# Hybrid attention/RWKV block on one core: the mixing's split weights kept in DRAM, loaded in a ring of three, and its stores on other queues

## The chip, the core and the metric

The kernel runs on one core of a Trainium2 chip. A core has a matrix engine (PE, whose weight loads are shown as PEld), a vector engine (DVE), a scalar engine (ACT), a general engine (POOL), and SP, which here only issues DMA transfers; ACT and POOL can issue them too. Each engine works through its own instructions in the order in which they were built, and waits where an operand is not there yet. The transfers of all issuers run on the same 16 DMA engines. The metric is the device time of one execution in microseconds (us). Three runs of the kernel before took 3460.87, 3462.41 and 3465.66 us.

## The reference

One layer over 2048 tokens of width 1024, in float32:

```python
h    = rms_norm(x, pre_mix_g)
proj = h @ w_in                      # 1536 attention, 1792 RWKV and 2048 gate columns
y_a  = chunk_band_attention(q, k, v, rel_bias)
y_b  = rwkv7_time_mix(p_rwkv, ...)   # recurrence over time, 8 heads of 64
merged = sigmoid(gate_a) * (y_a @ proj_a) + sigmoid(gate_b) * (y_b @ proj_b)
x = x + rms_norm(merged @ w_out, post_mix_g)
u = square(relu(rms_norm(x, pre_ffn_g) @ w_up)) @ w_down
x = x + rms_norm(u, post_ffn_g)
```

proj_a and proj_b are 512 x 1024, w_out is 1024 x 1024, w_up and w_down are 1024 x 4096 and 4096 x 1024.

## The kernel before

The tokens are cut into four groups of 512 (`G`). `run` (L1206) takes each group through `phase_rwkv`, `phase_attention` and `phase_merge`, which is called the mixing here, and then does the feed-forward part for two groups at a time (`phase_up`, `phase_down`).

**Precision.** A product is made of three: an operand is split into a rounded part `hi` and the rest `lo` (`split`, L68: a cast on ACT, a subtraction on DVE), and `mm3` (L72) adds hi x hi, hi x lo and lo x hi in PSUM. A block of 128 output columns for 512 tokens over 1024 inputs is thus 24 matmuls of 128x512.

**Weights of the mixing.** `wsplit` (L57) loads a block of weights raw through SP's queue (L62) and splits it (L69 on ACT writes `whi`, L70 on DVE writes `wlo`). Raw, hi and lo have two buffers each. It serves `dense` (L82: blocks of `w_in`, 14 for RWKV, 16 for the gates, 12 for attention), `branch` (L923: 8 blocks of `proj_b`, then 8 of `proj_a`, 256 KB each) and the loop over `w_out` in `phase_merge` (L955: 16 blocks of 256 KB). Each group does all of it anew: the same weights are loaded and split four times.

**The RWKV part.** `rwkv_pre` prepares a pair of heads, with one bonus product (L429) that waits for r (L427) and the products ps_A (L473). `rwkv_inverse` (L493) is a chain of 31 steps, two DVE instructions each (L506, L512), that ends with two transposes (L515, L517); `rwkv_blocks` starts with the products ps_t (L536), which wait for X of L515. Dense blocks of the gates (`gate`, L660) fill PE's time beside these chains. `mix` (L287) needs a carry column that POOL copies (L293, L294); `mN` (L394) is POOL's too.

**Stores and reloads.** Much is handed on through DRAM: the gates (`gd`, L665), the bonus (`bvd`, L431), the outputs of RWKV (`yd`, L658), keys and values for the next group (`kc`, `vc`, L797 and L798), branch b (`md`, L908), the mixing's output (`od`, L1231) and the residual's results (`x1`, L985; `ht`, L998; `td`, L1020). All of these go through SP's queue, among the loads.

**The merge.** `branch` loads a gate block `th` (L927, two buffers of 512 columns), multiplies y by a block of proj_a or proj_b (ps_p) and applies the gate on DVE (L932). Branch b is done beside the attention and stored in `md`; branch a then adds it back (`mb`, L946). After that come w_out's products (ps_o, L959), and beside them, as `between`, the norm of the next group (`phase_norm`, with transposes pstr, L115) and the residual of the group before (`residuals`, L968, with transposes ps_ht, L995). `rstd` (L91) runs on POOL.

**Order.** The program's order on each engine is not that of the source: when the program is built, instructions are ranked so that those whose inputs are expected earlier stand earlier. A change in one place thus moves instructions in others.

Of the kernel before, what the change touches and what calls it, by code (L numbers as in the profile page):

```python
# [17 lines left out]
P = 128  # L18
# [4 lines left out]
NP = 4  # L23
# [26 lines left out]
class Block:  # L50
# [31 lines left out]
    def dense(self, col):  # L82

        wh, wl = self.wsplit(
            self.a["w_in"][:, col : col + P].rearrange("(k p) n -> p k n", p=P), "w", KB, P
# [35 lines left out]
    def constants(self, ctx, mixing):  # L121
# [3 lines left out]
        dp = ctx.enter_context(tc.tile_pool(name="scratch", bufs=1, space=DRAM))  # L125
# [130 lines left out]
        self.gd = [dp.tile([P, G], F32, name=f"gd{i}") for i in range(2 * KB)]  # L256
        self.md = [dp.tile([P, G], F32, name=f"md{i}") for i in range(KB)]
# [81 lines left out]
    def rwkv_pre(self, g, p, rp, NA, between=lambda: None):  # L339
# [91 lines left out]
        nc.sync.dma_start(self.bvd[p], r)  # L431
# [192 lines left out]
    def rwkv_post(self, p, R):  # L624
# [33 lines left out]
        nc.sync.dma_start(self.yd[p], yf)  # L658

    def gate(self, i):  # L660
# [4 lines left out]
        nc.sync.dma_start(self.gd[i], t)  # L665
# [90 lines left out]
    def att_pair(self, g, p):  # L756
# [39 lines left out]
        if not lastg:  # L796
            nc.sync.dma_start(self.kc[p], KK[:, :, 1].bitcast(F32))  # L797
            nc.sync.dma_start(self.vc[p], VV[:, 1].bitcast(F32))  # L798
# [85 lines left out]
    def phase_attention(self, g):  # L884
# [5 lines left out]
        with ExitStack() as ctx:  # L890
# [16 lines left out]
            for i in range(KB):  # L907
                nc.sync.dma_start(self.md[i], self.branch(y, 1, i))  # L908
# [14 lines left out]
    def branch(self, y, br, i):  # L923

        nc, mp = self.nc, self.bp
        t = mp.tile([P, G], F32, tag="th", name="th")
        nc.sync.dma_start(t, self.gd[br * KB + i])  # L927
# [4 lines left out]
        nc.vector.scalar_tensor_tensor(t, t, 1.0, ps, op0=ALU.add, op1=ALU.mult)  # L932
        return t

    def phase_merge(self, g, o, between, early=iter(())):

        tc, nc, a = self.tc, self.nc, self.a
        with ExitStack() as ctx:
# [5 lines left out]
            for i in range(KB):  # L944
# [344 lines left out]
```

## Time and profile before

| | |
|---|---|
| median of three runs | 3462.41 us |
| profiled execution | 3462.33 us, of which the span from first to last instruction is 3460.6 us |
| mean granted TensorE clock | 0.985 |
| PE, PEld, DVE, ACT, POOL busy | 96%, 77%, 70%, 41%, 10% |
| DMA | 481.14 MB, 139 GB/s over the span |
| groups 0 to 3 of the mixing | about 0 to 520, 520 to 1060, 1060 to 1597, 1597 to 2118 us |
| feed-forward part | about 2118 to 3460 us |

The profile lists for each engine the busy time, and before what it sat idle. A row of the waits reads "who waits, in which line, for whom: us in total, times, longest". A row of a window gives, for a stretch of the span, each engine's busy time with its instructions, then the granted clock (1.00 is full), the DMA engines' mean busy share and the GB/s moved. A group of instructions is shown as line, engine, operation, "output<-inputs", shape and count, then busy time and mean ns of one, then the engine's idle time before them with what ended it. Matmuls are pipelined: one of 128x512 is shown with some 390 ns, though the next one starts some 0.23 us after it.

### The profile page before, as it was taken

To read this page: it belongs to the slowest core of one execution; us is meant where nothing else is said; L and a number is where in the kernel's file an instruction comes from. 1 tells how busy PE (TensorE), PEld (TensorE's weight loads), DVE (VectorE), ACT (ScalarE), POOL (GpSimd) and SP (SyncE) were. 2 spreads that over 40 slices of the span, in tenths; PEclk is the share of its full clock that TensorE was granted. 3 is DMA by queue.
4 is the path that set the end of the run, shared out by engine and by line. 5 is a ranking of instruction groups with operands and counts; after the bars stand their busy time and mean duration, and the time that the engine had idled before them with its cause. 6 is when DMAs were issued, how large, how long until landed. Compare 5 with 4: busy or idle time off the path is not lost. (4 is left out here: it accounts for less than half of the span.)

```text
span 3460.6 us, 50793 instructions
## 1 busy us (share of the span) xinstructions
PE 3310.7 (96%) x19233; PEld 2677.4 (77%) x19233; DVE 2421.3 (70%) x4206; ACT 1429.6 (41%) x2399; POOL 352.7 (10%) x700
## 2 busy tenths in 40 slices
PE   7999999999998999999999979999999999999998
PEld 5777777777877777877777867888888878888886
DVE  5774856766856765865774875777887788766667
ACT  4434634436644445644435635333331143331112
POOL 2210002100003110002210000111100021100001
PEclk9999999999999999999999999999999999999999
DMA  5223453225365225365224277334845374343333
GB/s 147 82 86 125 130 182 119 62 89 186 111 223 161 62 92 159 122 226 163 82 86 134 81 232 254 125 120 143 271 175 188 109 239 129 113 152 98 98 98 110
DMA packets 430124, 481.14 MB, mean 139 GB/s; under 512 B 19564, under 2 KB 322864, under 8 KB 429880
## 3 DMA queue, kind: packets, MB, share of 16 engines
q1 hardware_dynamic: 419640, 444.34, 40.2%
q0 software_dynamic: 10240, 33.56, 2.6%
q8 instruction: 151, 2.47, 0.3%
q14 instruction: 93, 0.76, 0.1%
HBM read 356.16 MB, written 124.81 MB: 139 GB/s over the span
## 5 line engine op out<-in xcount | busy, mean ns | idle before, releaser
L78 PE MATMUL ps_dn<-fop 128*128 128x512 f32 x3072 | 700.1, 390 | 0.9 <-DVE u L1169 0.9
L78 PEld LDWEIGHTS ps_dn<-fop 128*128 128x128 f32 x3072 | 575.9, 188 | 121.3 <-DVE u L1169 1.3
L78 PE MATMUL psd<-hh,whi 128*128 128x512 f32 x1344 | 546.4, 407 | 16.7 <-ACT whi L69 13.5
L78 PE MATMUL psd<-hl,whi 128*128 128x512 f32 x1344 | 544.9, 405 | 0.0
L78 PE MATMUL psd<-hh,wlo 128*128 128x512 f32 x1344 | 541.4, 403 | 0.7 <-DVE wlo L70 0.5
L69 ACT CAST whi<-wraw 128x1024 fp32r<-128x1024 f32 (+1 forms) x296 | 255.6, 864 | 578.2 <-PE psd L78 392.3
L70 DVE TENSOR_TENSOR wlo<-wraw,whi 128x1024 fp32r<-128x1024 f32 (+1 forms) x296 | 292.6, 989 | 264.9 <-ACT whi L69 200.4
L1169 DVE TENSOR_TENSOR u<-u,ps_dn 128x512 f32<-128x512 f32 x480 | 322.5, 684 | 152.8 <-PE ps_dn L78 152.0
L78 PEld LDWEIGHTS psd<-hh,whi 128*128 128x128 f32 x1344 | 258.3, 192 | 71.7 <-ACT whi L69 15.5
L78 PEld LDWEIGHTS psd<-hh,wlo 128*128 128x128 f32 x1344 | 258.0, 192 | 52.5 <-DVE wlo L70 3.5
L78 PEld LDWEIGHTS psd<-hl,whi 128*128 128x128 f32 x1344 | 258.6, 192 | 48.8
L69 ACT CAST fop<-wdraw 128x1024 fp32r<-128x1024 f32 x64 | 67.1, 1049 | 427.5 <-DVE u L1169 321.9
L1090 POOL DMA_DIRECT2D ad<-r x128 | 69.4, 543 | 683.8 <-DVE r L1089 683.8
L78 PE MATMUL ps_p<-yh,whi 128*128 128x512 f32 x256 | 107.8, 421 | 29.8 <-DVE th L932 17.8
L69 ACT CAST s12h<-s 128x1024 fp32r<-128x1024 f32 x32 | 33.7, 1054 | 185.1 <-PE ps_u L78 185.1
L826 DVE CUSTOM_DVE_ANT_0 sc<-bias,ps_s 128x640 f32<-128x640 f32 (+4 forms) x128 | 93.3, 729 | 22.4 <-PE ps_pt L838 13.0
L831 ACT ACTIVATE sc<-sc,mn 128x640 f32<-128x640 f32 (+4 forms) x128 | 97.8, 764 | 22.4 <-DVE mn L826 21.7
L78 PE MATMUL ps_p<-yh,wlo 128*128 128x512 f32 x256 | 105.4, 412 | 1.6 <-DVE wlo L70 1.6
L959 PE MATMUL ps_o<-whi,mh 128*128 128x512 f32 x256 | 98.6, 399 | 7.7 <-ACT whi L69 6.8
L78 PE MATMUL ps_p<-yl,whi 128*128 128x512 f32 x256 | 105.3, 412 | 0.0
L843 DVE TENSOR_TENSOR PTl<-ps_pt,PTh 128x640 fp32r<-128x640 f32 (+4 forms) x128 | 94.1, 735 | 12.9 <-ACT PTh L842 12.2
L959 PE MATMUL ps_o<-wlo,mh 128*128 128x512 f32 x256 | 102.1, 399 | 1.1 <-DVE wlo L70 1.1
(345 smaller groups left out, 6566.9 us busy)
## 6 DMA issues: line engine op xcount, KB each, us to landing
wraw<-in_w_in_dram SPq DMA_DIRECT2D x168, 512.0 KB
wraw<-in_w_up_dram SPq DMA_DIRECT2D x80, 512.0 KB
ad<-r POOLq DMA_DIRECT2D x128, 256.0 KB, 2.5
wdraw<-in_w_down_dram SPq DMA_DIRECT2D x64, 512.0 KB
araw<-ad SPq DMA_DIRECT2D x64, 512.0 KB
gd<-gate SPq DMA_DIRECT2D x64, 256.0 KB
th<-gd SPq DMA_DIRECT2D x64, 256.0 KB
wraw<-in_w_out_dram SPq DMA_DIRECT2D x64, 256.0 KB
```

The lines of the kernel that those rows point to most:

```text
L69: self.nc.scalar.copy(hi, src)
L70: self.nc.vector.tensor_tensor(lo, src, hi.bitcast(F32), ALU.subtract)
L78: mm = nc.tensor.matmul(ps, l, r, start=n == 0, stop=n == last).ins
L826: nc.vector.tensor_tensor_reduce(sc[:, 0:n], bias[:, s0:640], pss[:, c0 : c0 + n], 1.0, 3.0e38, ALU.add, ALU.min, mn,)
L831: nc.scalar.activation(sc[:, 0:n], sc[:, 0:n], AF.Exp, scale=-1.0, bias=mn, accum_out=sm)
L843: nc.vector.tensor_tensor(lv, pst[:, 0:nk], hv.bitcast(F32), ALU.subtract)
L959: nc.tensor.matmul(ps[t], l[:, k, ts], r[:, 0], start=k == 0 and j == 0, stop=k == KB - 1 and j == 2)
L1090: nc.gpsimd.dma_start(self.ad[fb][:, th], r)
L1169: nc.vector.tensor_tensor(u[t][:, ns], u[t][:, ns], ps, ALU.add)
```

## The change

Group 0 loads and splits each weight as before and in addition stores its two parts in DRAM (`kept`): hi through ACT's queue, lo through POOL's. Groups 1 to 3 load both parts with one transfer into one tile `w` and split nothing. All weight tiles now hold 1024 values a partition and part (`branches` makes two of the former blocks of 128 columns at once, the loop over w_out takes two blocks of rows), so that there are 58 of them in a group: 42 of w_in, 4 of proj_b, 4 of proj_a and 8 of w_out. The pool of the weights is opened after the first norm, with two buffers each of raw, hi and lo for group 0; it is closed before group 1 and opened again with three buffers of the double tile (24 KB a partition in both cases). Its buffers are released tile by tile.

The gate blocks, `md` and `mb` come in pairs too. The stores leave SP: bvd, yd, kc, vc, md, x1 and td go to POOL's queue, gd, od and ht to ACT's.

```diff
-    def wsplit(self, src, tag, k, n, raw_tag="raw", bufs=2):
+    def wsplit(self, src, k, n, key):
         nc = self.nc
-        w = self.wp
-        raw = w.tile([P, k, n], F32, tag=raw_tag, name="wraw")
+        if key in self.kept:
+            w = self.wp.tile([P, 2, k, n], F32R, tag="w", name="wsp")
+            nc.sync.dma_start(w.bitcast(F32), self.kept[key])
+            return w[:, 0], w[:, 1]
+        raw = self.wp.tile([P, k, n], F32, tag="raw", name="wraw")
         nc.sync.dma_start(raw, src)
-        hi = w.tile([P, k, n], F32R, tag=tag + "h", bufs=bufs, name="whi")
-        lo = w.tile([P, k, n], F32R, tag=tag + "l", bufs=bufs, name="wlo")
+        hi, lo = (self.wp.tile([P, k, n], F32R, tag="w" + x, name="w" + x) for x in ("hi", "lo"))
         self.split(hi, lo, raw)
+        d = self.kept[key] = self.dp.tile([P, 2, k, n], F32, name="kept_%s%d" % key)
+        nc.scalar.dma_start(d[:, 0], hi.bitcast(F32))
+        nc.gpsimd.dma_start(d[:, 1], lo.bitcast(F32))
         return hi, lo
...
-        self.gd = [dp.tile([P, G], F32, name=f"gd{i}") for i in range(2 * KB)]
-        self.md = [dp.tile([P, G], F32, name=f"md{i}") for i in range(KB)]
+        self.gd = [dp.tile([P, 2, G], F32, name=f"gd{i}") for i in range(KB)]
+        self.md = [dp.tile([P, 2, G], F32, name=f"md{i}") for i in range(KB // 2)]
...
-        nc.sync.dma_start(self.bvd[p], r)
+        nc.gpsimd.dma_start(self.bvd[p], r)
...
-        nc.sync.dma_start(self.gd[i], t)
+        nc.scalar.dma_start(self.gd[i // 2][:, i % 2], t)
...
-            for i in range(KB):
-                nc.sync.dma_start(self.md[i], self.branch(y, 1, i))
+            for i in range(KB // 2):
+                nc.gpsimd.dma_start(self.md[i], self.branches(y, 1, i))
...
-    def branch(self, y, br, i):
+    def branches(self, y, br, i):
-        nc, mp = self.nc, self.bp
-        t = mp.tile([P, G], F32, tag="th", name="th")
-        nc.sync.dma_start(t, self.gd[br * KB + i])
-        w = self.a[("proj_a", "proj_b")[br]][:, i * P : (i + 1) * P]
-        wh, wl = self.wsplit(w.rearrange("(k p) n -> p k n", p=P), "w", NP, P)
-        ps = self.pd.tile([P, G], F32, tag="d", name="ps_p")
-        self.mm3(ps, [(wh[:, k], wl[:, k], y[0][:, k], y[1][:, k]) for k in range(NP)])
-        nc.vector.scalar_tensor_tensor(t, t, 1.0, ps, op0=ALU.add, op1=ALU.mult)
+        nc = self.nc
+        t = self.bp.tile([P, 2, G], F32, tag="th", name="th")
+        nc.sync.dma_start(t, self.gd[br * KB // 2 + i])
+        w = self.a[("proj_a", "proj_b")[br]][:, 2 * i * P : (2 * i + 2) * P]
+        wh, wl = self.wsplit(w.rearrange("(k p) n -> p k n", p=P), NP, 2 * P, ("ab"[br], i))
+        for j in range(2):
+            c = slice(j * P, (j + 1) * P)
+            ps = self.pd.tile([P, G], F32, tag="d", name="ps_p")
+            self.mm3(ps, [(wh[:, k, c], wl[:, k, c], y[0][:, k], y[1][:, k]) for k in range(NP)])
+            nc.vector.scalar_tensor_tensor(t[:, j], t[:, j], 1.0, ps, op0=ALU.add, op1=ALU.mult)
         return t
...
-                advance(early, i % 2)
+                advance(early, 1)
...
                 for k in range(KB):
-                    wh, wl = self.wsplit(a["w_out"][k * P : (k + 1) * P, None, n * 512 : (n + 1) * 512], "w", 1, 512)
+                    if k % 2 == 0:
+                        rows = a["w_out"][k * P : (k + 2) * P, n * 512 : (n + 1) * 512]
+                        wh, wl = self.wsplit(rows.rearrange("(k p) n -> p k n", p=P), 2, 512, ("out", n * KB + k))
...
-            self.wp = e(tc.tile_pool(name="w", bufs=2))
...
+            weights = e(ExitStack())
             for g in range(self.NG):
+                if g < 2:
+                    weights.close()
+                    self.wp = weights.enter_context(tc.tile_pool(name="w", bufs=2 + g, reuse_waits="tile"))
...
-                        self.nc.sync.dma_start(self.od[g][t], o[t])
+                        self.nc.scalar.dma_start(self.od[g][t], o[t])
```

More of the change, by code (lines that the diff above doesn't have):

```diff
@@ L84, in dense @@
         wh, wl = self.wsplit(
-            self.a["w_in"][:, col : col + P].rearrange("(k p) n -> p k n", p=P), "w", KB, P
+            self.a["w_in"][:, col : col + P].rearrange("(k p) n -> p k n", p=P), KB, P, ("in", col)
         )
@@ L124, in constants @@
         cp = mixing.enter_context(tc.tile_pool(name="mconst", bufs=1, side="right"))
-        dp = ctx.enter_context(tc.tile_pool(name="scratch", bufs=1, space=DRAM))
+        dp = self.dp = ctx.enter_context(tc.tile_pool(name="scratch", bufs=1, space=DRAM))
+        self.kept = {}
         self.ident = keep.tile([P, P], F32, name="ident")
@@ L657, in rwkv_post @@
         nc.vector.tensor_tensor(yf, yf, ps, ALU.mult)
-        nc.sync.dma_start(self.yd[p], yf)
+        nc.gpsimd.dma_start(self.yd[p], yf)
     def gate(self, i):
@@ L796, in att_pair @@
         if not lastg:
-            nc.sync.dma_start(self.kc[p], KK[:, :, 1].bitcast(F32))
-            nc.sync.dma_start(self.vc[p], VV[:, 1].bitcast(F32))
+            nc.gpsimd.dma_start(self.kc[p], KK[:, :, 1].bitcast(F32))
+            nc.gpsimd.dma_start(self.vc[p], VV[:, 1].bitcast(F32))
         ya = ap.tile([P, G], F32, tag="ya", name="ya")
@@ L943, in phase_merge @@
             ml = cp.tile([P, KB, G], F32R, name="ml")
-            for i in range(KB):
-                mb = self.bp.tile([P, G], F32, tag="mb", name="mb")
+            for i in range(KB // 2):
+                mb = cp.tile([P, 2, G], F32, tag="mb", bufs=2, name="mb")
                 nc.sync.dma_start(mb, self.md[i])
-                t = self.branch(self.ya, 0, i)
+                t = self.branches(self.ya, 0, i)
                 nc.vector.tensor_tensor(t, t, mb, ALU.add)
-                self.split(mh[:, i], ml[:, i], t)
-                advance(early, i % 2)
+                self.split(mh[:, 2 * i : 2 * i + 2], ml[:, 2 * i : 2 * i + 2], t)
+                advance(early, 1)
             self.yctx.close()
@@ L959, in phase_merge @@
                             nc.tensor.matmul(
-                                ps[t], l[:, k, ts], r[:, 0], start=k == 0 and j == 0, stop=k == KB - 1 and j == 2
+                                ps[t], l[:, k, ts], r[:, k % 2], start=k == 0 and j == 0, stop=k == KB - 1 and j == 2
                             )
@@ L1019, in combinations @@
                 nc.vector.tensor_tensor(b[:, o], b[:, x], b[:, y], ALU.subtract)
-            nc.sync.dma_start(self.td[half][:, :, k], b)
+            nc.gpsimd.dma_start(self.td[half][:, :, k], b)
             yield
```

4 lines of the change are left out of this document (2 added, 2 removed).

## The prediction

> **What bounds the kernel now.** I read the page's head first, then the windows of the four groups, then who PE waited for in groups 1 to 3, then the instructions that the change removes.
>
> ```profile
> span 3460.6 us, 50793 instructions
> PE 3310.7 (96%) x19233; PEld 2677.4 (77%) x19233; DVE 2421.3 (70%) x4206; ACT 1429.6 (41%) x2399; POOL 352.7 (10%) x700
> ```
> ```profile
> 0.00:520.00 520.00, 481.50 (x3189) 379.48 (x3190) 336.76 (x742) 241.35 (x462) 61.67 (x130) 0.98 0.40 125
> 520.00:1060.00 540.00, 517.25 (x3488) 414.99 (x3487) 364.01 (x709) 271.64 (x482) 65.19 (x129) 0.99 0.43 138
> 1060.00:1597.00 537.00, 507.84 (x3431) 406.85 (x3430) 360.93 (x704) 266.44 (x476) 61.57 (x128) 0.98 0.42 136
> 1597.00:2118.00 521.00, 482.77 (x3284) 385.07 (x3283) 350.24 (x696) 242.79 (x429) 47.14 (x97) 0.96 0.42 132
> 2118.00:3460.60 1342.60, 1321.37 (x5847) 1091.04 (x5845) 1009.40 (x1358) 407.40 (x554) 117.10 (x216) 1.00 0.45 149
> ```
> The columns of the windows are length, then busy time of PE, PEld, DVE, ACT and POOL, the granted clock, the DMA share and GB/s. PE is the bound at 96%. The last row is the feed-forward part, which the change reaches only through the queue of a few stores; at full clock I leave it at nothing. The first four rows are the groups of the mixing. No other engine is near full there: DVE 64.8% to 67.4%, DMA 0.40 to 0.43. So the removal of work on ACT and DVE pays only where PE waited for it, or where the clock was lowered behind a wait. In groups 1 to 3 the clock rows give 0.01 x 540 + 0.02 x 537 + 0.04 x 521 = 37 us of clock time not granted (rounded rows: some 8 us either way).
>
> ```profile
> PE ps_t L536 <- DVE X L515: 18.5, 6, 3.4
> PE ps_p L78 <- DVE th L932: 13.2, 8, 3.1
> PE ps_p L78 <- ACT whi L69: 11.7, 2, 6.1
> PE ps_ht L995 <- DVE xn L990: 8.0, 4, 2.1
> PE psd L78 <- ACT whi L69: 7.0, 2, 3.7
> PE ps_o L959 <- ACT whi L69: 6.3, 6, 2.8
> PE ps_bonus L429 <- DVE r L427: 6.1, 6, 1.2
> PE ps_p L78 <- DVE wlo L70: 1.6, 2, 0.9
> PE ps_o L959 <- DVE wlo L70: 1.1, 5, 0.2
> ```
> These are PE's waits between 520 and 2118 us, all three groups together: total, times, longest. They and ten smaller rows sum to 87.5 us. That and the 37 us of clock are the ceiling of any gain: 124 us.
>
> **The change part by part. Removed: the splits of groups 1 to 3.**
>
> ```profile
> L70 DVE TENSOR_TENSOR wlo<-wraw,whi 128x1024 fp32r<-128x1024 f32 (+1 forms) x220 | 217.6, 989 | 190.5 <-ACT whi L69 142.3 <-ACT SV L580 34.7 <-PE ps_yt L644 12.6
> L69 ACT CAST whi<-wraw 128x1024 fp32r<-128x1024 f32 (+1 forms) x221 | 190.8, 864 | 428.5 <-PE psd L78 291.5 <-PE ps_o L959 37.6 <-DMA wraw<-in_w_out_dram 33.4
> ```
> So 218 us of DVE and 191 us of ACT go (the window cuts off one or two). Where does PE see it? First at ps_t, which waits for the serial chain of the inverse on DVE (L506, L512). Splits stand inside that chain; the two rows are group 1's first and second inverse, from 605.4 to 635.2 and from 710.5 to 737.5 us:
>
> ```profile
> L70 DVE TENSOR_TENSOR wlo<-wraw,whi 128x1024 fp32r<-128x1024 f32 x6 | 7.3, 1211 | 0.0
> L70 DVE TENSOR_TENSOR wlo<-wraw,whi 128x1024 fp32r<-128x1024 f32 x4 | 4.9, 1220 | 0.0
> ```
> The chain gets 7.3 and 4.9 us shorter. In the changed program's order PE has 124 dense matmuls instead of 133 ahead of the first ps_t, and 117 instead of 114 ahead of the second. In the feed-forward row a matmul takes 1342.6 / 5847 = 0.230 us, so PE arrives 2.1 us sooner and 0.7 us later. The longest wait is 3.4 us: 3.4 + 2.1 - 7.3 and 3.4 - 0.7 - 4.9 are both below zero. The whole row goes: 18.5 us. The lower bound is half of it, if other DVE work moves into the holes.
>
> The waits on whi and wlo themselves: psd 7.0 us, twice, where a group starts and ACT and DVE are busy with the residuals. The parts need neither engine, so I take it all. ps_p and ps_o together are 11.7 + 1.6 + 6.3 + 1.1 = 20.7 us, almost all of it in group 3's merge, where DMA is busy too (below); I take half, 10.3. The next thing late there is the part's own load.
>
> th (13.2 us) is DVE waiting for gate blocks that SP loads two blocks ahead, behind stores. With pairs of blocks in two buffers they are four ahead; I take half, 6.6. Of the other 28.1 us, waits for chains that stay, I take 3 (between 0 and 28). Together 18.5 + 7.0 + 10.3 + 6.6 + 3.0 = 45.4 us.
>
> **The clock.** Behind a ps_t wait the clock falls:
>
> ```profile
> PE ps_t L536 <- DVE X L515: 2.8, 1, 2.8
> ```
> ```profile
> 632.00:644.00 12.00, 9.21 (x150) 6.78 (x149) 11.05 (x20) 8.06 (x14) 1.40 (x3) 0.86 0.15 45
> ```
> The wait is the only one between 630 and 650 us; the clock of the window around it is 0.86, or 1.7 us not granted. In proportion to the waits removed, 45.4 / 87.5 of 37 us is 19; some of that runs while PE idles anyway, so I take 15 (0 to 37). Gain: 60 us.
>
> The Trainium skill (TensorE: Matmul & The Clock Gate, Part 1: The HAM clock gate) has the clock halve only after at least one idle window of about 3.4 us. By that rule the removal of waits of 3 us would win next to no clock and the sum below would be 3437. The row above, a lowered clock after a wait of 2.8 us, speaks against the rule, and I keep the 15; 3437 stays inside the forecast's own range.
>
> **Added: parts written once, read three times.** There are 42 + 8 + 8 = 58 of them (dense, projections in pairs, w_out in pairs), 512 KB as read before and 1 MB as kept: 1.05 MB x 58 = 61 MB of writes in group 0, and 174 loads of double size afterwards.
>
> ```profile
> 160.00:200.00 40.00, 39.77 (x482) 31.85 (x481) 20.15 (x44) 18.24 (x40) 4.46 (x11) 1.00 0.12 35
> 2136.00:2144.00 8.00, 8.00 (x37) 6.63 (x36) 8.00 (x9) 7.54 (x10) 0.80 (x2) 1.00 1.02 397
> q1 hardware_dynamic: 419640, 444.34, 40.2%
> ```
> In the first window there is hardly anything but w_in, in short rows: 35 / 0.12 = 292 GB/s when all engines are busy. In the second long rows move: 397 / 1.02 = 389. The whole hardware queue gives 444.34 MB / (0.402 x 3460.6 us) = 319. A kept part is contiguous and so nearer to 389: 2.7 us (3.3 at 319) where 0.52 MB took 1.8. Per load 0.9 to 1.5 us more of the DMA engines; over a group 52 to 87 us on some 225 busy ones of 530, which is 52 to 59%. That hides, on average. It must also hide in the merges:
>
> ```profile
> 435.00:480.00 45.00, 39.76 (x173) 31.15 (x172) 33.03 (x50) 20.26 (x35) 4.11 (x10) 0.96 0.76 240
> 480.00:520.00 40.00, 40.00 (x178) 32.56 (x177) 12.32 (x18) 14.26 (x24) 0.00 (x0) 1.00 0.34 105
> 930.00:990.00 60.00, 53.52 (x270) 43.03 (x270) 44.33 (x77) 29.83 (x56) 5.79 (x11) 0.97 0.71 228
> 2016.00:2075.00 59.00, 41.11 (x158) 30.52 (x157) 36.20 (x57) 12.80 (x23) 0.00 (x0) 0.88 0.84 275
> ```
> Group 1's projections hold 0.71 x 60 = 43 us of transfers; eight parts add 7 to 12, so 50 to 55 of 60. Group 3 holds 50 of 59 and gets 4 to 6 more. Both stay under, but without room for bunching: I charge 2 us each in groups 1 and 2, 3 us in group 3, 7 in all (0 to 21). In group 0, 435 to 480 us holds 34 us and gets 8 x 2.7 = 22 of stores: 56 in 45. The stretch to 520 us has 26 us free and eight more parts, 22 us. The backlog can slide, the first part of it cannot: I charge 10 us (0 to 25).
>
> **Moved: stores from SP to ACT and POOL.**
>
> ```profile
> SPq L665 <- ACT gate L664: 227.9, 42, 18.5
> 945.15 0.32 SPq L927 DMA_DIRECT2D th<-gd  x1
> L1090 POOL DMA_DIRECT2D ad<-r x128 | 69.4, 543 | 683.8 <-DVE r L1089 683.8
> ad<-r POOLq DMA_DIRECT2D x128, 256.0 KB, 2.5
> ```
> SP stood 228 us, in groups 1 to 3, in front of gate stores with loads queued behind; that goes. An issue is 0.32 us on SP and 0.54 on POOL. ACT gets 16 gd, 8 ht and 4 od a group, 28 x 0.32 = 9 us where 64 us of casts went, each behind its own instruction, so it waits for nobody; in group 0 also 58 hi stores, 19 us on an engine with 279 us idle. POOL gets bvd, yd, kc, vc, md and x1 (24 a group, 13 us, td besides in group 3) and in group 0 the 58 lo stores, 31 us of 458 idle. But it waits for DVE there: behind a waiting store stand the carry copies (L293), mN (L394) and rstd (L96), on which mix, the BR products and the norms wait. I charge 3 us (0 to 9). L62's ring: before, two raw tiles and two split ones; after, three whole parts, so SP waits for PE instead of DVE. Two dense blocks take 2 x 24 x 0.230 = 11 us, and a part needs the 2.5 us of a landing and some 3 of bytes: no charge outside the merges.
>
> The Trainium skill (DMA: Bandwidth & Descriptors, Issuing engines are not separate DMA queues) says that spreading transfers over engines saves only the issue time. By that rule the 6.6 us of th and some 2 of clock fall away and the sum is 3431, again inside the forecast's own range. The L665 row is a wait of an in-order queue for data, which the rule leaves out.
>
> **Sum.** 60 - 10 - 7 - 3 = 40 us. The profiled execution took 3462.3 (its span and 1.7 around it), 0.1 from the median of 3462.4: 3422. Own range: the ps_t row halved, no clock beyond 5 and merges at 20 instead of 17 give 3445; all clock gives 3400.
>
> **The rivals.** (1) *Transfers become the bound in the merges of all four groups.* It decides where a 1 MB load or the store of a part takes longer than the 11 us that two blocks cover. Then the halves of whi and th with their clock (10.3 + 6.6 + 6 = 23) aren't won, group 0 pays 25, and the three other merges 10 each: 60 - 23 - 25 - 30 - 3 = -21, 3483. For it: 0.84 in group 3 and 56 us of demand in 45 in group 0. Against: windows that reach 1.02 at 397 GB/s with PE at 8.00 of 8.00. (2) *Nothing comes of it:* PE's order is fixed, and behind ps_t another chain is late at once (X feeds L543 to L603); 7.0 + 10.3 + 6.6 and 8 of clock remain, less charges of 30: 3460. Against: DVE loses a fifth of its work. (3) *Everything late on ACT and DVE disappears:* all 87.5 and 25 of clock, less 22: 3372. Against: ps_ht and ps_bonus wait for chains without a split.
>
> **How the numbers follow.** Chances: forecast 0.58, rival 1 0.15, rival 2 0.11, rival 3 0.16. The predicted time is 3422; the likeliest case's own range 3400 to 3445. For 8 in 10 the range reaches to most of rival 3 and the milder half of rival 1: 3380 to 3470. A measurement of this kernel tells 0.2% (7 us) from no change. Faster: 0.58 + 0.16 and a little of rival 2, 0.76; same: the rest of it, 0.09; slower: 0.15.
>
> **What would show it.** Right: no ps_t wait above 1 us in groups 1 to 3, and clock 0.99 or more there; DVE some 70 us less busy in each; group 0 longer by some 10 us, and its DMA share near 0.7. Wrong: PE waiting for loads of the kept parts by name, a group 0 longer by 25 us, or POOL's stores in front of carry copies that PE's chain waits for.

## The result, and the profile after

| | before | changed |
|---|---|---|
| median of four runs | 3464.03 us (3460.87 to 3469.59) | 3505.44 us (3502.44 to 3508.79) |
| ratio, 95% interval | | 1.012 (1.0107 to 1.0133) |
| mean granted TensorE clock | 0.985 | 0.975 |
| moved by DMA | 481.14 MB | 633.14 MB |

The changed kernel is slower by 1.2%, 41 us; 3422 was predicted. The head of its page, with busy times and DMA queues:

```profile
span 3500.7 us, 50013 instructions
PE 3312.1 (95%) x19233; PEld 2685.9 (77%) x19233; DVE 2230.5 (64%) x3936; ACT 1250.0 (36%) x2145; POOL 416.9 (12%) x854
q1 hardware_dynamic: 220984, 455.85, 39.3%
q0 software_dynamic: 31392, 110.12, 8.1%
q10 hardware_dynamic: 36768, 63.97, 4.9%
```

The work did go: DVE has 191 us less to do and ACT 180. PE, the bound, does the same 19233 matmuls in 3312 us, and its idle time grew. The windows of the changed kernel, cut where about as many matmuls have run as at the cuts of before (length, busy PE, PEld, DVE, ACT, POOL, clock, DMA share, GB/s):

```profile
0.00:543.00 543.00, 482.88 (x3190) 383.11 (x3191) 334.54 (x717) 237.43 (x441) 105.49 (x208) 0.95 0.67 232
543.00:1088.00 545.00, 513.67 (x3477) 413.81 (x3475) 297.55 (x621) 208.12 (x399) 67.63 (x153) 0.97 0.56 200
1088.00:1632.00 544.00, 507.78 (x3428) 409.74 (x3428) 297.78 (x621) 207.48 (x398) 66.16 (x152) 0.96 0.54 191
1632.00:2150.00 518.00, 486.28 (x3312) 391.19 (x3313) 286.79 (x616) 186.23 (x355) 49.45 (x113) 0.97 0.52 181
2150.00:3500.70 1350.70, 1321.45 (x5830) 1088.04 (x5828) 1013.83 (x1361) 410.75 (x556) 128.16 (x228) 0.99 0.45 149
```

Against 520, 540, 537, 521 and 1342.6 us that is +23, +5, +7, -3 and +8. Group 0 lost most. Groups 1 to 3, which were to gain, lost 9 together although DVE is 63 to 66 us less busy in each. The DMA share rose from 0.40 to 0.67 in group 0 and by 0.10 to 0.13 in the others, and the clock fell everywhere but in group 3. PE's waits in groups 1 to 3 of the changed kernel (543 to 2150 us):

```profile
PE ps_ht L1006 <- DVE xn L1001: 20.3, 4, 5.6
PE ps_s L827 <- DVE mn L833: 18.2, 3, 6.8
PE ps_p L84 <- DMA wsp<-kept_a: 14.2, 3, 8.1
PE ps_yt L651 <- ACT yf L656: 13.9, 3, 4.6
PE pstr L121 <- DVE xn L290: 7.9, 2, 4.8
PE psd L84 <- ACT lw L302: 5.8, 2, 3.0
PE ps_t L550 <- ACT Z L545: 3.9, 3, 1.3
PE ps_p L84 <- DVE th L941: 0.5, 2, 0.3
```

The 18.5 us of ps_t behind X are gone, as are the waits for whi and wlo, and th fell from 13.2 to 0.5. Where they were, other waits stand, most of them rows that were small or absent before: ps_ht 20.3 (8.0 before), ps_s 18.2, ps_yt 13.9, and 14.2 for the parts themselves.

### The profile page after: what moved, and what is told of

Its sections match the earlier page's. It is cut to its first block, busy times and chain, and to the rows that moved or that the text cites. A ratio compares the mean times of both kernels' runs of the same rounds, so it can differ in the third digit from the quotient of the medians.

```text
span 3500.7 us, 50013 instructions
## 1 busy us (share of the span) xinstructions
PE 3312.1 (95%) x19233; PEld 2685.9 (77%) x19233; DVE 2230.5 (64%) x3936; ACT 1250.0 (36%) x2145; POOL 416.9 (12%) x854
## 2 busy tenths in 40 slices
DMA packets 289382, 633.14 MB, mean 181 GB/s; under 512 B 19372, under 2 KB 164976, under 8 KB 266872
## 5 line engine op out<-in xcount | busy, mean ns | idle before, releaser
L84 PE MATMUL ps_dn<-fop 128*128 128x512 f32 x3072 | 701.3, 390 | 3.6 <-DVE u L1180 3.5
L84 PE MATMUL psd<-hh,wsp 128*128 128x512 f32 x2016 | 679.6, 405 | 6.7 <-ACT lw L302 5.8
L84 PEld LDWEIGHTS ps_dn<-fop 128*128 128x128 f32 x3072 | 575.5, 188 | 125.7 <-DVE u L1180 5.8
L84 PEld LDWEIGHTS psd<-hh,wsp 128*128 128x128 f32 x2016 | 382.8, 192 | 85.4 <-ACT lw L302 6.6
L84 PE MATMUL psd<-hl,wsp 128*128 128x512 f32 x1008 | 407.5, 404 | 0.0
L84 PEld LDWEIGHTS psd<-hl,wsp 128*128 128x128 f32 x1008 | 193.5, 192 | 35.3
L84 PE MATMUL psd<-hh,whi 128*128 128x512 f32 x336 | 138.9, 413 | 16.9 <-ACT whi L75 15.8
L84 PE MATMUL ps_p<-yh,wsp 128*128 128x512 f32 x384 | 133.2, 413 | 14.6 <-DMA wsp<-kept_a 14.2
L84 PE MATMUL psd<-hl,whi 128*128 128x512 f32 x336 | 137.2, 408 | 0.0
L84 PE MATMUL psd<-hh,wlo 128*128 128x512 f32 x336 | 137.0, 408 | 0.1
L970 PE MATMUL ps_o<-wsp,mh 128*128 128x512 f32 x384 | 120.4, 395 | 1.8 <-DMA wsp<-kept_out 1.3
L833 DVE CUSTOM_DVE_ANT_0 sc<-bias,ps_s 128x640 f32<-128x640 f32 (+4 forms) x128 | 93.9, 733 | 38.5 <-PE ps_pt L845 22.5
L1099 ACT ACTIVATE r<-r 128x512 f32<-128x512 f32 x128 | 80.7, 630 | 52.2 <-DVE r L1098 51.9
```

The source lines that it names most:

```text
L84: mm = nc.tensor.matmul(ps, l, r, start=n == 0, stop=n == last).ins
L833: nc.vector.tensor_tensor_reduce(sc[:, 0:n], bias[:, s0:640], pss[:, c0 : c0 + n], 1.0, 3.0e38, ALU.add, ALU.min, mn,)
L970: nc.tensor.matmul(ps[t], l[:, k, ts], r[:, k % 2], start=k == 0 and j == 0, stop=k == KB - 1 and j == 2)
L1099: nc.scalar.activation(r, r, AF.Relu)
```

## The experiments

All ratios are to runs of the kernel before on the same chip. A step between two runs is the difference of their ratios times 3464 us; its uncertainty is the root of the sum of squares of the two half intervals. The account that came out of them stands first, the runs follow.

| run | edit | median us | ratio (95%) |
|---|---|---|---|
| e5 | pairs alone | 3439.56 | 0.9920 (0.9905 to 0.9935) |
| e13 | and all ten stores moved | 3446.61 | 0.9942 (0.9926 to 0.9957) |
| e3 | and the late pool of the weights | 3464.37 | 0.9986 (0.9977 to 0.9996) |
| e6 | and the parts stored, not read | 3489.76 | 1.0063 (1.0046 to 1.0079) |
| e7 | and read instead of split, half of each | 3480.53 | 1.0036 (1.0024 to 1.0048) |
| changed | and read whole | 3505.44 | 1.012 (1.0107 to 1.0133) |

So the 41 us are: pairs -28 (5 either way), moved stores +8 (7), late pool +15 (6), storing the parts +27 (7), no splits in groups 1 to 3 -9 (7), loads of double size +29 (6). The step to e7 puts more than the splits aside: the ring of three and one contiguous transfer a part come with it.

**The first four: one part undone or alone.** My first theory, from the trace after, was that the moved stores did it: on POOL's queue five of the seven land 5.6 to 7.3 us after issue (medians; bvd 2.4, vc 2.9), and SP and ACT wait for landings.

All ten stores back on SP, the parts kept (e1):

```diff
-        nc.gpsimd.dma_start(self.x1[g][ts], x)
+        nc.sync.dma_start(self.x1[g][ts], x)
...
-                nc.scalar.dma_start(self.ht[g][:, h * 4 : h * 4 + 4, ts], f)
+                nc.sync.dma_start(self.ht[g][:, h * 4 : h * 4 + 4, ts], f)
```

> The changed kernel with its ten moved stores (bvd, yd, gd, kc, vc, md, x1, ht, td, od) issued by SP again; the parts are still kept, by ACT and POOL, and loaded in the ring of three. Theory S (the moved stores cost the time: they land 5 to 8 us after issue on POOL's queue instead of about 2.5, and reloads, buffers and ACT wait for them): the attention of groups 1 to 3 gets back 5.6 + 6.2 + 6.8 us, the feed-forward part 8 to 11, group 0 some 6, so about 3505 - 40 = 3465, between 3455 and 3475. Theory K (the loads and stores of the kept parts cost it: 61 MB of writes and the doubled loads crowd the DMA engines): 3490 to 3505, with the waits on ps_s and at the boundary still there. Theory B (the pool of the weights that opens only after the first norm, and what follows from it): 3500 or more.

Measured 3523.93, ratio 1.016 (1.0142 to 1.0179): slower still by 14 us. It lies 49 us above the range of theory S and 19 above that of K. SP's waits between 480 and 575 us, and PE's between 540 and 570, at the end of group 0 show why SP is a worse place beside kept parts:

```profile
SPq L1245 <- ACT o L976: 22.0, 4, 21.1
```
```profile
PE psd L84 <- DMA wsp<-kept_in: 9.4, 1, 9.4
```

SP stands 21.1 us in front of the first store of od until ACT has copied o; behind it in SP's order stand the first parts of group 1, and PE then waits 9.4 us for one. When group 0's matmuls are done (the 3190th starts), this run is 17 us behind the changed kernel, 560.5 against 543.1 us.

The ten stores alone, on the kernel before (e2):

```diff
-        nc.sync.dma_start(self.bvd[p], r)
+        nc.gpsimd.dma_start(self.bvd[p], r)
...
-                        self.nc.sync.dma_start(self.od[g][t], o[t])
+                        self.nc.scalar.dma_start(self.od[g][t], o[t])
```

> The kernel before with nothing but the ten stores moved, as the change moves them: no parts kept, no pairs, its own pool of the weights. Theory S: slower than before by most of what the changed kernel lost in the attention, at the boundary and in the feed-forward part, 20 to 35 us, so 3485 to 3500. Theory K: SP is free of its waits for the gate stores, 3450 to 3464. Theory B: 3464.

Measured 3479.84, 1.0038 (1.0026 to 1.005): they cost, but 13 us, not 20 to 35; that lies between the ranges of S and K.

No parts kept, the rest as changed (e3):

```diff
-        if key in self.kept:
-            w = self.wp.tile([P, 2, k, n], F32R, tag="w", name="wsp")
-            nc.sync.dma_start(w.bitcast(F32), self.kept[key])
-            return w[:, 0], w[:, 1]
...
-        d = self.kept[key] = self.dp.tile([P, 2, k, n], F32, name="kept_%s%d" % key)
-        nc.scalar.dma_start(d[:, 0], hi.bitcast(F32))
-        nc.gpsimd.dma_start(d[:, 1], lo.bitcast(F32))
...
-                if g < 2:
+                if g < 1:
```

> The changed kernel without the kept parts: every group loads its weights raw and splits them on ACT and DVE, in two buffers each; the pairs, the moved stores and the late pool of the weights stay. Theory S: the stores still cost, and the splits come back on DVE ahead of ps_t (3.3 us a group) and in the merges (3 to 4 us a group): 3515 to 3530. Theory K: 3464 to 3475, as no part is written or loaded at double size. Theory B: 3510 or so.

Measured 3464.37, 0.9986 (0.9977 to 0.9996). That is the foot of theory K's range and 50 below S's: keeping the parts costs 46 us (6 either way), with all splits back. S fell as the main cause.

The first group's pool opened before the first norm, parts kept (e4):

```diff
+            weights = e(ExitStack())
+            self.wp = weights.enter_context(tc.tile_pool(name="w", bufs=2, reuse_waits="tile"))
...
-                if g < 2:
+                if g == 1:
```

> The changed kernel with the first group's pool of the weights opened before the first norm, in memory of its own, as the kernel before has it. Theories S and K: the start gets back the 7 to 8 us that the first psd comes late, and no more: 3495 to 3499. Theory B: 20 us or more come back, 3485 or less. If the start is made up for later anyway: 3505.

Measured 3502.4, 1.0096 (1.0075 to 1.0116): 8 us less by the ratios (8 either way), 3 by the medians, between the ranges of 3495 to 3499 and of 3505, so it decides nothing. Without kept parts the late pool costs 15 (e3 against e13). What it does at the start is seen in the issues of the first raw weights in the first 46 us (durations of an issue in ns, then first and last start), of before and of the changed kernel:

```profile
L62 SPq DMA_DIRECT2D wraw<-in_w_in_dram x5: 367/415/1368, 14.3 to 45.7; - x5
```
```profile
L66 SPq DMA_DIRECT2D wraw<-in_w_in_dram x3: 412/423/3842, 24.8 to 34.8; - x3
```

The first norm's pool is closed before the weights' is opened, and the first load leaves at 24.8 instead of 14.3 us. PE's busy time of the 46 us from 14 to 60 falls from 37.14 to 28.45; with the early pool of e4 it is 31.79.

The larger part shows elsewhere. From e13 to e3 the 100th matmul comes 6.5 us later (51.1 and 57.6 us), and the first thousand matmuls of the feed-forward part take 238.7 instead of 228.1 us, with a wait of PE of 5.4 us for ACT's `bh` that e13 lacks. Those thousand take 234.4 to 241.5 us in all ten runs whose weights have the pool in the new form, e4 and the changed kernel (236.2 and 236.1) among them, and 228.0 to 228.5 in the ten that open it once before the first norm. e4, which still opens a pool again before group 1, could thus not win this part back. What in the pool delays `bh` was not tested.

**Stores, bytes, or SP's order.** The pairs alone, with before's pool and SP's stores (e5; from the change come `branches`, the pairs of `gd`, `md`, `mb`, and the loop over w_out; from e3 the cut in `wsplit`; and, against the changed kernel):

```diff
+            self.wp = e(tc.tile_pool(name="w", bufs=2))
             self.hp = e(tc.tile_pool(name="h", bufs=1))
...
-                if g < 2:
-                    weights.close()
-                    self.wp = weights.enter_context(tc.tile_pool(name="w", bufs=2 + g, reuse_waits="tile"))
```

> Only the pairing of the change: blocks of the projections and rows of w_out in pairs, gd and md in pairs; the weights are split in every group, in the pool of before (opened before the first norm), and all ten stores stay on SP. If the merges gain by the pairs themselves, as in the run without kept parts (-7.4, -7.8, -8.3 and -11.7 us by the marks of PE), and the moved stores (13 us) and the late pool (8) are spared: 3425 to 3445. If the pairs gained only because SP was free of the stores: 3455 to 3465.

Measured 3439.56, 0.992 (0.9905 to 0.9935): inside the first range. The pairs win by themselves.

The parts stored by group 0 and never read (e6):

```diff
         self.split(hi, lo, raw)
+        if key in self.kept:
+            return hi, lo
         d = self.kept[key] = self.dp.tile([P, 2, k, n], F32, name="kept_%s%d" % key)
```

> The run without kept parts plus their stores: the first group stores all 58 parts, but no group reads them, every group splits anew. If the stores cost what group 0 lost (about 15 us between its start and the merge, by PE's marks): 3475 to 3485, and all of it in group 0. If only the loads of double size cost: 3464 to 3468.

Measured 3489.76, 1.0063 (1.0046 to 1.0079), 5 us above the range I gave to the stores. Two windows of group 0, without the stores (first fence, e3) and with them (second, e6):

```profile
60.00:120.00 60.00, 57.79 (x294) 45.83 (x293) 40.98 (x64) 24.28 (x40) 17.75 (x28) 1.00 0.31 97
320.00:360.00 40.00, 37.52 (x182) 29.32 (x181) 28.02 (x66) 24.22 (x53) 4.47 (x18) 1.00 0.53 165
```
```profile
60.00:120.00 60.00, 57.79 (x286) 45.77 (x285) 41.32 (x63) 25.87 (x41) 22.97 (x37) 1.00 0.71 239
320.00:360.00 40.00, 34.19 (x152) 27.60 (x151) 17.64 (x29) 17.54 (x31) 6.87 (x22) 0.91 0.85 286
```

At a share of 0.71 PE's 57.79 us are untouched, and from the 100th matmul to the 500th both runs take 84 us. At 0.85, where the attention adds its own loads, PE loses 3 us of 40 and the clock falls to 0.91 (the second windows are not at quite the same place of the program). The chain behind that loss, from the timelines of DVE, ACT and PE in e6 (start, duration, in brackets the idle time before and what ended it):

```profile
340.82 0.69 DVE L659 TENSOR_TENSOR yf<-yf,bv 128x512 f32<-128x512 f32 x1 [4.92 <-DMA bv<-bvd]
...
344.05 0.68 DVE L783 SCALAR_TENSOR_TENSOR QA<-psd,QA 64x512 fp32r<-64x512 f32 x1
```
```profile
344.76 0.59 ACT L780 ACTIVATE QA<-psd 64x512 fp32r<-64x512 f32 x1 [5.88 <-DVE QA L783]
...
346.47 1.04 ACT L73 CAST whi<-wraw 128x1024 fp32r<-128x1024 f32 x1
```
```profile
347.54 0.77 PE L82 MATMUL psd<-hh,whi 128*128 128x512 f32 x1 [5.68 <-ACT whi L73]
```

A reload of 256 KB, bv, is late; DVE stands in front of it, so QA comes late for ACT, ACT comes late to whi, and PE waits 5.7 us. In e3 DVE waits 2.5 us there in all. This is one place of several. PE's waits over the whole run that differ most, in e3 (first fence) and in e6:

```profile
PE ps_t L536 <- DVE X L515: 26.8, 8, 3.9
PE ps_p L77 <- DVE th L934: 8.4, 4, 3.0
```
```profile
PE ps_t L541 <- DVE X L520: 32.6, 8, 7.7
PE ps_p L82 <- DVE th L939: 17.9, 5, 8.2
```

The waits for whi at psd grow as well, from 11.2 to 20.1 us. So the cost is not spread evenly: e6 is 2 us behind e3 at the 500th matmul, 15 at the 2000th and at the first of the projections, and 24 at the end of group 0. 15 us of it are lost ahead of the place where I had put it, in the RWKV part and the attention, and 9 in that place, the projections, where a gate block th is late.

Half of each part loaded, in the same ring of three (e7; the upper half stands in for the lower one, which isn't loaded):

```diff
-            nc.sync.dma_start(w.bitcast(F32), self.kept[key])
-            return w[:, 0], w[:, 1]
+            nc.sync.dma_start(w[:, 0].bitcast(F32), self.kept[key][:, 0])
+            return w[:, 0], w[:, 0]
```

> The changed kernel with half of each kept part loaded in groups 1 to 3: the upper half stands in for the lower one in the products, so a load is 512 KB as before, in the same ring of three. Bytes (the doubled loads crowd the DMA engines, other loads and stores land late behind them): 3470 to 3480, the 6 us of each attention and 4 us of each merge are back. Order (SP stands in front of a part until PE gives a tile free, and what it issues behind it comes late): 3495 to 3505.

The same in six tiles of half the size (e8):

```diff
-            w = self.wp.tile([P, 2, k, n], F32R, tag="w", name="wsp")
+            w = self.wp.tile([P, k, n], F32R, tag="w", name="wsp")
...
-                    self.wp = weights.enter_context(tc.tile_pool(name="w", bufs=2 + g, reuse_waits="tile"))
+                    self.wp = weights.enter_context(tc.tile_pool(name="w", bufs=2 + 4 * g, reuse_waits="tile"))
```

> The same half loads in a ring of six tiles of half the size, in the same memory: SP runs three parts further ahead of PE. Bytes: within 3 us of the ring of three with half loads. Order: 20 us or more below it.

Measured 3480.53, 1.0036 (1.0024 to 1.0048), and 3478.17, 1.0029 (1.0018 to 1.0039). Bytes, not order: halving them wins 29 us, and three more parts of lead win nothing that can be told (2 us, 6 either way). SP's long wait in front of the ring, which the trace shows (`SPq L63 <- PE psd L84`, 761 us), costs nothing that a longer ring would win back. In the first heads of the attentions of groups 1 to 3, the changed kernel (first fence) and half loads (second):

```profile
835.00:865.00 30.00, 23.90 (x132) 19.76 (x131) 18.43 (x42) 17.18 (x34) 2.32 (x8) 0.89 0.68 251
1376.00:1406.00 30.00, 22.21 (x125) 18.52 (x123) 18.07 (x44) 16.62 (x33) 1.18 (x4) 0.89 0.63 231
1917.00:1947.00 30.00, 24.23 (x131) 20.11 (x130) 18.89 (x44) 16.77 (x34) 0.66 (x4) 0.89 0.55 208
```
```profile
838.00:868.00 30.00, 29.04 (x159) 23.61 (x159) 20.93 (x47) 20.02 (x39) 1.53 (x4) 0.98 0.57 198
1373.00:1403.00 30.00, 29.81 (x174) 24.23 (x174) 24.86 (x55) 21.68 (x42) 1.82 (x6) 1.00 0.58 197
1905.00:1935.00 30.00, 29.89 (x172) 23.98 (x171) 25.06 (x55) 21.86 (x43) 0.29 (x2) 1.00 0.50 163
```

PE is busy 5.1, 7.6 and 5.7 us less in 30, beside a share that averages only 0.55 to 0.68. The windows are not at quite the same place of the program. Counted by PE's matmuls in order of start, the changed kernel falls behind half loads by 3.5, 4.4 and 3.6 us in these stretches (the 5200th matmul to the 5500th, the 8700th to the 9000th, the 12200th to the 12500th), and by 4.4, 4.5 and 4.5 at the ends of groups 1 to 3 (6400th to 6670th, 9600th to 10100th, 13100th to 13400th): 11.5 and 13.4 us, which together are the 24.7 us between the two profiled executions (what lies between cancels).

What is late in the first heads is vr, the reload of the values of the group before, 512 KB that SP issues at 833.59 us behind a part of 1 MB. ACT, DVE and PE in the changed kernel, and ACT with half loads (second fence):

```profile
842.12 1.04 ACT L775 CAST VV<-vr 128x1024 fp32r<-128x1024 f32 x1 [6.55 <-DMA vr<-vc]
843.36 0.29 DVE L802 TENSOR_TENSOR VV<-ps_vt,VV 128x128 fp32r<-128x128 f32 x1 [6.87 <-ACT VV L801]
844.44 0.63 PE L827 MATMUL ps_s<-KK,QA 128*128 128x320 f32 x1 [5.88 <-DVE mn L833]
```
```profile
840.96 1.05 ACT L775 CAST VV<-vr 128x1024 fp32r<-128x1024 f32 x1 [2.58 <-DMA vr<-vc]
```

ACT stands at the copy of vr; DVE's VV needs ACT's next copy, and DVE's sc (L833), which frees a buffer of ps_s, stands behind it. ACT stands there for 6.55, 7.45 and 6.21 us in the three groups, and PE's three waits of 5.9, 6.8 and 5.6 us behind it are the row of 18.2 us. With half loads ACT stands for 2.58, 1.89 and 1.91, and PE waits at ps_s 6.8 us in all, for another instruction (ACT's KK, L772). At the ends of the groups the rows that differ are pstr's 7.9 us (none with half loads), ps_p's wait for the parts (14.2, with half loads still 11.0) and ps_ht (20.3 and 17.4).

Stores are late beside the parts too, though not all. The DMA issues of the changed kernel and of half loads (KB each, median us from issue to landing):

```profile
kc<-KK POOLq DMA_DIRECT2D x12, 512.0 KB, 5.6
yd<-yf POOLq DMA_DIRECT2D x16, 256.0 KB, 5.6
```
```profile
kc<-KK POOLq DMA_DIRECT2D x12, 512.0 KB, 4.2
yd<-yf POOLq DMA_DIRECT2D x16, 256.0 KB, 2.4
```

The 256 KB of bvd land in 2.4 us in both. SP waits for landings as well: before the load of the attention's bias (L886) it stands for yd 7.4, 7.2 and 7.4 us in the three groups, and with half loads in groups 2 and 3, 5.0 and 4.3 us. Its largest such wait, for x1's stores before xr is loaded (L989, 52.1 us), is not of this kind: with half loads it is 55.4.

**Which of the stores.** The upper halves alone stored (e11), and the lower halves alone (e12), neither read:

```diff
         nc.scalar.dma_start(d[:, 0], hi.bitcast(F32))
-        nc.gpsimd.dma_start(d[:, 1], lo.bitcast(F32))
```
```diff
-        nc.scalar.dma_start(d[:, 0], hi.bitcast(F32))
         nc.gpsimd.dma_start(d[:, 1], lo.bitcast(F32))
```

> The run that stores the parts and doesn't read them, with the upper halves alone stored (ACT's queue, 30 MB); the lower halves are not kept. Bytes: half of what both cost over the run without kept parts, so 3474 to 3480. POOL's software queue as the cause: 3464 to 3468.

> The same with the lower halves alone stored (POOL's queue, 30 MB); the upper halves are not kept. Bytes: 3474 to 3480, as with the upper halves. POOL's software queue as the cause: 3484 to 3490.

Measured 3469.79, 1.0012 (1.0003 to 1.0022), and 3476.24, 1.0029 (1.0017 to 1.004): over e3, 9 us (5 either way) for ACT's 30 MB and 15 (5) for POOL's. The first lies between its two ranges, the second in that of bytes. Neither is free and they add up to nearly the 27 of both; POOL's is the dearer one by 6 us (5 either way), and not the whole, as the queue theory wanted.

The x1 store alone moved, on top of the pairs (e10), and the nine others (e9). The line of e10 against e5:

```diff
-            nc.sync.dma_start(self.x1[g][ts], x)
+            nc.gpsimd.dma_start(self.x1[g][ts], x)
```

> Pairs alone, with only the store of x1 moved to POOL. If x1 is the cost: 3450 to 3458, with the waits on ps_ht at the ends of groups 1 and 2 grown by some 9 us each before part of it is made up. If not: 3437 to 3445.

> Pairs alone, with nine of the ten stores moved as the change moves them; x1 stays on SP. If the moved x1 is what the stores cost (the residuals reload xr only when the x1 store has landed, and the group boundary and the feed-forward part come late): 3437 to 3445, as with pairs alone. If the cost is spread over all stores of POOL: 3448 to 3455.

Measured 3437.73, 0.9918 (0.9903 to 0.9933), and 3440.56, 0.9923 (0.9905 to 0.9941): the same as the pairs alone, both. e9 would have fitted x1 as the cause; e10 shows that x1 alone costs nothing. All ten with the pairs in the early pool (e13), POOL's seven without ACT's three (e14), and the changed kernel with ACT's three back on SP (e15). ACT's three against SP, as e13 stands to e14:

```diff
-        nc.sync.dma_start(self.gd[i // 2][:, i % 2], t)
+        nc.scalar.dma_start(self.gd[i // 2][:, i % 2], t)
...
-                nc.sync.dma_start(self.ht[g][:, h * 4 : h * 4 + 4, ts], f)
+                nc.scalar.dma_start(self.ht[g][:, h * 4 : h * 4 + 4, ts], f)
...
-                        self.nc.sync.dma_start(self.od[g][t], o[t])
+                        self.nc.scalar.dma_start(self.od[g][t], o[t])
```

> Pairs alone with all ten stores moved, in the early pool: the run without kept parts but for its late pool. If the late pool cost 8 us and the x1 store beside the others the rest of the difference: 3452 to 3458. If the late pool set off all of it: 3438 to 3444.

> Pairs alone with the seven stores of POOL moved (bvd, yd, kc, vc, md, x1, td) and the three of ACT (gd, ht, od) left on SP. If ht and od on ACT's queue hold up the residuals at the end of groups 1 and 2: no loss there (9 us and 8 us before part is made up, with nine moved), 3434 to 3440. If POOL's stores do it: the loss stays, 3445 or more.

> The changed kernel with the three stores of ACT (gd, ht, od) back on SP. If the stores in ACT's order made ACT late for ps_yt and Z: the three ps_yt waits of 4.6 us are gone as in the run with all ten stores back, about 15 us less, 3488 to 3495, unless SP in front of the gate stores takes it back. If SP's order takes it back, as with all ten stores back: 3505 to 3524.

e13: 3446.61, between the two ranges given; e3, which has the late pool besides, is 15 us (6 either way) above it. e14: 3429.42, 0.9886 (0.9865 to 0.9906), below its range. POOL's seven stores win 12 us (9 either way) over the pairs alone; ACT's three lose 19 (9) on top. e15: 3503.54, 1.0101 (1.0085 to 1.0117), between its two ranges. The ps_yt waits are gone from its list, as expected of the order on ACT, but PE waits 9.1 us for a part behind od on SP, as in e1, and 14.4 us for ps_vt, which had no such row: the sum is 7 us below the changed kernel, 7 either way.

Then each of these three lines alone, on top of e14:

> Pairs and POOL's seven stores as in the fastest run so far (3429), with ht alone moved to ACT. If ht, which follows each copy hf in the residuals, is the cause: 3440 to 3448, with ps_ht waiting 12 us at the end of group 1. If not: 3425 to 3434.

> The same with od alone moved to ACT (four stores of 512 KB at each group's end, which on SP stand in front of the next group's loads). If od is the cause, as its stores then run beside those loads: 3440 to 3448. If not: 3425 to 3434.

> The same with gd alone moved to ACT (16 stores a group behind the gates). If gd is the cause: 3440 to 3448. If SP is freed of the gate stores, as my prediction had it: 3420 to 3428.

ht: 3444.37, 0.9936 (0.9912 to 0.996), +17 us (11 either way). od: 3455.72, 0.9966 (0.9955 to 0.9978), +28 (8), above the range given. gd: 3422.95, 0.9868 (0.9847 to 0.9889), -6 (10 either way), the lowest median of all and in the range of SP set free, though not told from e14 by the intervals. The three add up to 39 us and all together cost 19; the difference has an uncertainty of its own size, so whether ht and od cost less in company is barely told. ACT at the end of group 1 with od moved (e17; start, duration, and in brackets the idle time before and what ended it):

```profile
1037.21 0.33 ACTq L1235 DMA_DIRECT2D od<-o  x1
...
1045.21 0.58 ACT L1001 COPY hf<-ps_ht 128x512 f32<-128x512 f32 x1 [5.98 <-DMA ht<-hf]
...
1053.84 0.58 ACT L1001 COPY hf<-ps_ht 128x512 f32<-128x512 f32 x1 [4.73 <-DMA ht<-hf]
```

hf has two buffers, and its next copy waits until an ht store has landed; here that takes 6.0 and 4.7 us while od's 512 KB stores run on the other queue (1.7 and 1.5 at the same place in e14, where SP sends od and ht one after the other). Behind the copy stand ACT's xn and sqo of the next tile, on which DVE's xn and PE's ps_ht hang. PE's ps_ht row in e14, in e17, and in e13 with all three moved:

```profile
PE ps_ht L999 <- DVE xn L994: 9.6, 6, 3.2
```
```profile
PE ps_ht L999 <- DVE xn L994: 31.0, 5, 8.1
```
```profile
PE ps_ht L999 <- DVE xn L994: 26.1, 5, 6.9
```

So ps_ht is where both runs lose. But ACT's stand is not the only way there: in e13, where ACT issues both od and ht, it waits for ht only 2.0 us in the whole run. There the reload of xr is late, as SP waits up to 7.5 us for the store of x1 in its buffer to land. And in e16, where ACT stands 15.2 us for ht, ps_ht is 10.5. Which of the ways costs how much was not tried.

The same stand of ACT is in the changed kernel: 32.6 us at hf for ht, ten times, and 23.8 at the gates for gd:

```profile
ACT hf L1008 <- DMA ht<-hf: 32.6, 10, 7.4
ACT gate L671 <- DMA gd<-gate: 23.8, 5, 4.8
```

**A version that beats both.** e18 keeps the pairs, before's pool and the splits, moves POOL's seven stores and gd, and leaves ht and od on SP: 0.9868, 46 us below before and 87 below the changed kernel by the ratios. e14, with gd on SP too, is as good within the noise.

## Why the prediction was wrong

*What bounds it, and the ps_t waits: right, and worth little.* PE stayed the bound. The X waits went in all three groups, as the step worked out (3.4 + 2.1 - 7.3 below zero). But "the whole row goes: 18.5 us" counted a wait as won time. In the changed kernel ps_yt's 13.9 and Z's 3.9 us took its place. Rival 2 named this (another chain is late at once), and was given 0.11. With ACT's three stores back on SP (e15) the ps_yt waits vanish, so these stores in ACT's order made them; but 14.4 us at ps_vt stand in their place, and little is won.

*whi, wlo and th: the waits went, the gain was not theirs.* psd's 7.0 us, ps_p's and ps_o's went, and "the next thing late there is the part's own load" came true with 14.2 us in group 3, more than the 11.7 + 1.6 us of whi and wlo that had stood at ps_p. th fell to 0.5. But th and the merges are won by the pairs, in e5, without a part kept: 28 us, the largest gain of the whole change, which the prediction had only as 6.6 for th. In e5 the waits for th in groups 1 to 3 are 2.2 us instead of 13.2, while those for whi at ps_p (13.4) and psd (11.5) stay; no run shows where the rest of the 28 comes from. All splits of groups 1 to 3, 409 us of two engines, were worth 9 us (7 either way) in e7 against e6, the ring and the contiguous loads included.

*The clock: wrong in sign.* +15 was predicted; the mean fell from 0.985 to 0.975. The share of waits removed was the wrong measure, as each new wait lowers it again: 0.89 in the attention windows above, with PE 22 to 24 of 30 us busy. The Trainium skill (TensorE: Matmul & The Clock Gate, Part 1: The HAM clock gate) has the clock halve after an idle window of about 3.4 us; the waits on ps_s, 5.6 to 6.8 us, are longer than that, so the 0.89 beside them agrees with it and does not test it for the shorter waits that were weighed.

*"That hides, on average": this step failed.* The bytes of the doubled loads were priced in the merges alone, 7 us; they cost 29 (6 either way). The sum of 52 to 59% of the DMA engines is right (0.52 to 0.56 measured), and the conclusion isn't. The share says how much is moved, not how long a small transfer stands behind 1 MB parts. The attention, where vr, kr and bias go between the parts, was not looked at, and about half of the loss lies there (11.5 of 24.7 us between the profiled executions), behind vr; the other half lies at the ends of the groups, 13.4 us where 7 were charged.

*Group 0's stores: mis-sized, and only in part in their place.* 10 us (0 to 25) were charged from 435 to 520 us; they cost 27 (7). PE's first ps_p starts at 418.0 us in e3 and at 433.2 in e6: 15 us were lost before the projections began. Some 9 more followed in the stretch that was named, near the 10 charged.

*Moved stores, 3 us (0 to 9): wrong in its parts.* "Each behind its own instruction, so it waits for nobody" left out that a later instruction needs the buffer, which is free only when the store has landed: ACT waited 32.6 us for ht and 23.8 for gd. ht and od on ACT cost 17 (11 either way) and 28 us (8) alone. What I feared, POOL's stores in front of the carry copies, won 12 (9) instead; gd on ACT, where SP was to be set free, gives -6 (10), which can't be told from nothing. The Trainium skill (DMA: Bandwidth & Descriptors, Issuing engines are not separate DMA queues) says that transfers of all engines interleave and that spreading them saves only issue time. Its first half agrees with yd, whose stores on POOL's queue land in 5.6 us beside SP's loads of 1 MB and in 2.4 beside loads of 512 KB; that nothing but issue time is at stake, the runs do not bear out: the same od stores cost 28 us by the engine alone that issues them.

*Not priced at all: the pool opened late.* The diff shows that `wp` moves behind the first norm; that costs 15 us (6 either way) without kept parts, some 7 of it at the start and the rest at the head of the feed-forward part, which the prediction left at nothing. In the changed kernel the first thousand matmuls of that part take 236.1 us, 228.0 before.

*The sum.* Gain predicted 60, measured 37 (28 and 9); charges predicted 20, measured 79 (27, 29, 8 and 15). Rival 1, transfers as the bound, had the right resource and sign, at 3483; its charges of 25 for group 0 and 30 for the later groups are near the 27 and 29 measured, though it put all of them in the merges, and the 28 won by the pairs and the 23 of pool and stores it did not have.

*Still open.* How ht and od on ACT come to cost what they do, alone and together, and what in the late pool delays the feed-forward part, wasn't tried. That vr is late because it lands behind a part is read from the trace; the runs show that halving the parts removes most of its wait.

## What to carry to other kernels

Work taken off engines that are not the bound is worth its share of the bound's waits at most, and here 409 us of ACT and DVE bought 9; bytes put in their place cost several times that with the DMA engines half idle on average. Before transfers are added, look at the stretches where small loads feed the bound, and at what waits for a landing there. A store moved to a compute engine can make that engine wait for landings where its buffer is needed again soon: count the buffers of the tile against the landing time under load, and move such stores one by one, as ht and od cost here and gd did not. A pool that is opened at another place is a change of its own: look at the start and at the head of the next phase.

## What the runs showed of the hardware that was not expected

The stores of yd, 256 KB on POOL's queue, land in 2.4 us (median) beside loads of 512 KB (e7) and in 5.6 beside loads of 1 MB (changed kernel), while bvd's, of the same size and on the same queue, land in 2.4 in both. PE is untouched at a share of the DMA engines of 0.71 over 60 us of the RWKV part (e6), and is busy a fifth less than with half loads at 0.55 to 0.68 over 30 us where it hangs on reloads. So the mean share did not tell here which stretch would lose.
